# Early loads and early sums for the last product of a layer's last projection pair

## The chip, the cores and the metric

The kernel runs on one core of a Trainium2 chip. The metric is device time in microseconds (us) of one execution, shown as the median of several runs.

## The reference

Two layers of a streaming encoder on 512 tokens of width 2048, in float32:

```
def hybrid_layer(x, ...):
    h = rmsnorm(x, g_pre)
    z = h @ w_in                       # columns for a GLA group and an attention group
    o_gla = silu(gg) * rmsnorm(gla_chunk_causal(gq, gk, gv, log_a), g_gla)
    o_att = silu(ag) * rmsnorm(chunk_band_attention(aq, ak, av, rel_bias), g_att)
    y = concatenate([o_gla, o_att]) @ w_out
    return x + rmsnorm(y, g_post)
```

`reference` applies this twice. The change lies in `y = ... @ w_out` of the first layer, in its last two blocks of 512 columns, and so just ahead of the second layer's first projection.

## The kernel before

Weights come in blocks of 512 columns, each cut into eight chunks of 128 x 1024 float32 (512 KB). Every chunk is split into a rounded high half `wh` (cast on ScalarE, L200) and a low half `wl` (subtraction on VectorE, L209), so that three fast matmuls give nearly float32 accuracy.

Most blocks are multiplied in pairs by a Strassen-like scheme (`fast_gemm`): seven products P1 to P7 take the place of eight. Each product is a row of four jobs, one for each chunk index c from 0 to 3. A job is 12 matmuls of 128x512. The order in which the jobs run is written out by hand; for this pair it is `PROD_END`, where "20" is P2's job 0:

```
PROD_END = order("10 20 11 21 12 22 13 23 50 51 60 52 61 53 62 63 30 31 32 33 70 71 72 73 40 41 42 43")
```

A `Job` has three steps, each prepared some jobs ahead (`ahead`: up to five for loads, up to four for the others):

- `load` sends DMAs from SyncE's queue (SP). P1 loads into the ring `H` (4 buffers); P2, P5, P6 and, in this pair, P4 load into the ring `raw` (5 buffers). P5, P6, P3 and P7 also fetch an operand (a sum of activations, hi and lo half) into the ring `sa` (4 buffers), at L180. In the first layer's last pair (`mid`), P6 also loads the chunk that P7 will need into the slots `a110` to `a113`, under `p["t", c]`.
- `high` makes the weight combination on VectorE: `h = h + r` in place for P5, P6 and P4 (L194), `r = h - r` for P7 (L196). Then ScalarE casts the result to `wh`.
- `low` subtracts `wh` from it into `wl` (ring of 3 buffers).

`slot(tag, ...)` gives a named buffer that is held by one tile at a time; a new tile of the same tag waits for the last reader of the one before. P2's operands in this pair lie in the slots `a120`, `a121`, `g14` and `g15` (`OG` for p = 0): P2's jobs 0 to 3 read `g14`, `g15`, `a120`, `a121`.

The tile framework orders each engine's instructions ahead of time; `tc.issue_after(x)` puts an instruction behind x on its engine. Side work is written as generators that `pump` advances between jobs: in this stage `finish(0)` and `prep_half`. When P3 is complete, `finish_both` reduces the squares (L1372), takes the inverse root on GpSimd (L429), updates the residual rows on VectorE (L1383, four of them) and stores them to `x_mid`. `prep_half` then takes the squares (L442), reduces them (L443), scales the rows (L497, L499; its scaled rows lie in `g0`, `g14`, `g1`, `g15`), transposes them on TensorE (L513) and builds the second layer's operands. P4's last job is put behind the second group of transposes. The jobs behind P4 are the second layer's first block, of kind `std`; each loads one chunk into `raw`.

Of the kernel before, what the change touches and what calls it, by code (L numbers as in the profile page):

```python
# [11 lines left out]
ALU = mybir.AluOpType  # L12
# [11 lines left out]
NB_IN = 14  # L24
# [9 lines left out]
def hybrid_trunk(  # L34
# [13 lines left out]
    nc = tc.nc  # L48
# [16 lines left out]
    def nm(s):  # L65
        serial[0] += 1
        return f"{s}_{serial[0]}"

    def slot(tag, shape, dtype=F32):
        return slots.tile([P] + shape, dtype, tag=tag, name=nm(tag))  # L70

    def rtile(tag, shape=(2, W), dtype=F32, bufs=4):
        return ring.tile([P] + list(shape), dtype, tag=tag, name=nm(tag), bufs=bufs)
# [27 lines left out]
    def flat(t):  # L101
        return t.bitcast(F32).rearrange("p a b -> p (a b)")
# [30 lines left out]
    PROD_OUT = order("10 20 11 21 12 13 50 51 60 61 22 23 52 53 62 63 30 31 32 33 70 71 72 73 40 41 42 43")  # L133
    LEFT = {"P5": "S1", "P6": "S2", "P3": "S4", "P7": "S3", "P4": "A22"}
    SPARE = ("g12", "g13", "g16", "g17")
    lows, last_turn = [], [None]
    last_cast, last_low, last_mm, last_load, last_h = [None], [None], [None], [None], [None]

    class Job:
# [14 lines left out]
        def load(self):  # L154
            k, c, p, b0, b1 = self.kind, self.c, self.pair, self.b0, self.b1
            end = b0 >= NB_IN and k != "std"
            if end:
                c = OC[c]
            top, bottom = (c + 4, c) if end else (c, c + 4)
            mid = end and b0 == W23[0] and self.l < L - 1  # L160
            if k == "std":
                self.raw = self.fetch(rtile("raw", bufs=5), b0, c)
            elif k == "P1":
                p["H", self.c] = self.fetch(rtile("H"), b0, top)
                last_h[0] = last_load[0]
            elif k == "P5":
                p["r", self.c] = self.fetch(rtile("raw", bufs=5), b1, top)
            elif k == "P6":
                p["r", self.c] = self.fetch(rtile("raw", bufs=5), b1, bottom)
            elif k == "P7":  # L170
                p["r", self.c] = p.pop(("t", self.c), None) or self.fetch(rtile("raw", bufs=5), b0, top)
            elif k == "P2" or (k == "P4" and end):
                p["r", self.c] = self.fetch(rtile("raw", bufs=5), b0, bottom)
            sums = (so_d if end else sa_d)[self.l]
            src = sums.get((LEFT.get(k), c))
            if src is not None and b0 != NB_IN and not (k == "P5" and b0 == AV0):
                until(lambda: k == "P4" or (id(sums), LEFT[k], c) in written)
                self.a = rtile("sa", (2, 512), F32R)
                with tc.issue_after(last_h[0]) if mid else nullcontext():
                    last_load[0] = nc.sync.dma_start(flat(self.a), src).ins  # L180
            if b0 == W23[0] and k == ("P6" if mid else "P5"):
                with tc.issue_after(last_h[0]):
                    p["t", self.c] = self.fetch(slot(f"a11{self.c}" if mid else SPARE[self.c], [2, 512]), b0, c + 4)

        def high(self):
            k, c, p = self.kind, self.c, self.pair
            if k == "std":
                src = self.raw
            else:
                h, r = p["H", c], p.get(("r", c))  # L190
                src = h if k in ("P1", "P5", "P6", "P4") else r
                with tc.issue_after(lows[-2]) if self.b0 >= NB_IN else nullcontext():
                    if k in ("P5", "P6") or (k == "P4" and self.b0 >= NB_IN):
                        nc.vector.tensor_tensor(out=h, in0=h, in1=r, op=ALU.add)  # L194
                    elif k == "P7":
                        nc.vector.tensor_tensor(out=r, in0=h, in1=r, op=ALU.subtract)  # L196
            self.src = src
            self.wh = rtile("wh", dtype=F32R)
            for z in self.parts():
                last_cast[0] = nc.scalar.copy(self.wh[:, z, :], src[:, z, :]).ins  # L200
# [70 lines left out]
    def until(cond):  # L271
        while not cond():
            assert tasks or delayed
            pump(1)
# [1234 lines left out]
```

## Time and profile before

| | us |
|---|---|
| median of 3 runs | 1618.36 (1616.69 to 1619.23) |
| the profiled execution | 1617.52 |
| its span, first to last instruction | 1615.5 |

The page of the profile lists busy time by engine, a picture of the span in 40 slices, the chain of work that ended last and the costliest groups of instructions. A row of the timeline reads: start, duration, engine, line, operation, output<-input, form, count, and in brackets the idle time before it with what ended it. A row of stretches reads: stretch, its length, busy time (and instruction count) of PE (matmul), PEld (weight load), DVE (VectorE), ACT (ScalarE) and POOL (GpSimd), the granted TensorE clock, the DMA engines' busy share, and GB/s. A row of DMA issues gives the output and input, the queue, the count, the size of each and the median time from issue to landing. A row of waits gives total us, times, and the longest.

In this trace the first layer's last pair runs on PE from about 725 us (P1 and P2) over 747 (P5 and P6), 769 (P3), 780 (P7) and 791 (P4) to about 806 us.

### The profile page before, as it was taken

The numbers are of one execution on the slowest core, as the hardware profiler recorded it, in microseconds if no ns is written. First come the engines' busy times: TensorE is split into PE (matmuls) and PEld (weight loads), VectorE is DVE, ScalarE is ACT, GpSimd is POOL, SyncE is SP. The second block draws the span as 40 slices with busy tenths as digits, with TensorE's granted clock in tenths as the row PEclk, the third lists the DMA queues.
The fourth block names the chain that finished last, engine by engine and source line by source line (L and its number), as shares of the span: only waits on it lengthen the run. The fifth ranks groups of instructions, "written<-read, shape, count | busy, mean of one in ns | idle before, by whom it ended". The sixth has DMA issues, their size and how long they took to land.

```text
span 1615.5 us, 24476 instructions
## 1 busy us (share of the span) xinstructions
PE 1600.5 (99%) x8938; PEld 1372.8 (85%) x8938; DVE 1272.4 (79%) x1646; ACT 918.5 (57%) x1507; POOL 131.5 (8%) x192
## 2 busy tenths in 40 slices
PE   9999999999999999999999999999999999999997
PEld 7888999998888777888788889999988887788886
DVE  5977778678777878998988677786786878689887
ACT  7544445657455546665696444456675545566654
POOL 0120000010010010100122000000100100101001
PEclk9999999999999999999999999999999999999999
DMA  9797686685867768689779886867858687686986
GB/s 370 263 366 268 240 293 216 226 299 176 286 211 277 268 217 317 223 307 381 265 263 359 330 295 228 305 203 243 309 201 294 208 298 254 222 302 233 342 299 193
DMA packets 133928, 438.17 MB, mean 271 GB/s; under 512 B 14404, under 2 KB 27204, under 8 KB 133776
## 3 DMA queue, kind: packets, MB, share of 16 engines
q1 hardware_dynamic: 117072, 375.99, 66.9%
q0 software_dynamic: 16160, 59.53, 10.0%
q8 instruction: 71, 1.16, 0.3%
q10 hardware_dynamic: 576, 1.08, 0.2%
q14 instruction: 49, 0.40, 0.1%
HBM read 377.02 MB, written 61.62 MB: 272 GB/s over the span
## 4 chain that ended last, share of the span: by engine, by line
PE 94%; DVE 2%; DMA 1%; issue 1%; ACT 1%; POOL 0%; DVEq 0%; SPq 0%; ACTq 0%; POOLq 0%
PE mm L387 53%; PE mm L377 19%; PE mm L309 10%; PE ax L937 2%; PE ax L387 2%; PE ax L1123 1%; PE ax L920 1%; PE ax L744 1%; PE ax L1095 1%; DMA raw<-in_w_dram 1%; PE ax L900 1%; PE ax L899 1%; PE ax L898 1%; DVE wl L209 0%; DMA bias<-in_rel_dram 0%
## 5 line engine op out<-in xcount | busy, mean ns | idle before, releaser
L387 PE MATMUL mm<-wh,sa 128*128 128x512 f32 x1600 | 517.8, 394 | 0.8 <-ACT wh L200 0.5
L200 ACT CAST wh<-H 128x1024 fp32r<-128x1024 f32 x256 | 268.5, 1051 | 217.0 <-PE mm L387 91.6
L209 DVE TENSOR_TENSOR wl<-H,wh 128x1024 fp32r<-128x1024 f32 x256 | 312.3, 1221 | 94.6 <-PE mm L387 37.6
L387 PEld LDWEIGHTS mm<-wh,sa 128*128 128x128 f32 x1600 | 299.5, 188 | 73.0 <-issue 9.4
L200 ACT CAST wh<-raw 128x1024 fp32r<-128x1024 f32 (+1 forms) x233 | 244.1, 1052 | 197.0 <-PE mm L387 89.5
L209 DVE TENSOR_TENSOR wl<-raw,wh 128x1024 fp32r<-128x1024 f32 (+1 forms) x233 | 282.4, 1215 | 61.9 <-PE mm L387 24.5
L387 PE MATMUL mm<-wl,sa 128*128 128x512 f32 x800 | 312.6, 391 | 0.0
L377 PE MATMUL mm<-sa,wh 128*128 128x256 f32 x1280 | 237.4, 285 | 0.0
L387 PE MATMUL mm<-wh,a 128*128 128x512 f32 x640 | 211.5, 394 | 0.0
L377 PEld LDWEIGHTS mm<-sa,wh 128*128 128x128 f32 x1280 | 200.3, 191 | 0.3
L377 PE MATMUL mm<-sa,wl 128*128 128x256 f32 x640 | 180.9, 283 | 0.0
L387 PEld LDWEIGHTS mm<-wl,sa 128*128 128x128 f32 x800 | 150.3, 188 | 30.1 <-DVE wl L209 0.4
L194 DVE TENSOR_TENSOR H<-H,raw 128x1024 f32<-128x1024 f32 x144 | 174.9, 1219 | 1.0
L387 PEld LDWEIGHTS mm<-wh,a 128*128 128x128 f32 x640 | 119.5, 188 | 24.9
L387 PE MATMUL mm<-wl,a 128*128 128x512 f32 x320 | 125.6, 393 | 0.0
L377 PEld LDWEIGHTS mm<-sa,wl 128*128 128x128 f32 x640 | 122.5, 191 | 0.0
L429 POOL TENSOR_TENSOR sm<-sm,mhalf 128x2 f32<-128x2 f32 (+2 forms) x40 | 55.5, 1387 | 764.3 <-DVE sm L947 458.7
L196 DVE TENSOR_TENSOR raw<-H,raw 128x1024 f32<-128x1024 f32 x56 | 68.5, 1223 | 51.1 <-DMA raw<-in_w_dram 50.5
L387 PE MATMUL mm<-wh,g 128*128 128x512 f32 x320 | 101.6, 391 | 0.0
L377 PE MATMUL mm<-a,wh 128*128 128x256 f32 x512 | 95.4, 285 | 0.0
L339 ACT COPY ev<-mm 128x512 f32<-128x512 f32 x104 | 60.7, 584 | 60.2 <-PE mm L387 43.4
L215 DVE TENSOR_TENSOR H<-H,raw 128x1024 f32<-128x1024 f32 x48 | 58.7, 1223 | 35.7 <-DMA raw<-in_w_dram 35.4
(250 smaller groups left out, 2323.8 us busy)
## 6 DMA issues: line engine op xcount, KB each, us to landing
raw<-in_w_dram SPq DMA_DIRECT2D x311, 512.0 KB, 5.2
sa<-S SPq DMA_DIRECT2D x184, 512.0 KB, 4.5
H<-in_w_dram SPq DMA_DIRECT2D x64, 512.0 KB, 5.0
sa<-A SPq DMA_DIRECT2D x48, 512.0 KB, 5.8
S<-g POOLq DMA_DIRECT2D x32, 512.0 KB, 8.7
sa<-oS SPq DMA_DIRECT2D x32, 512.0 KB, 5.3
oS<-g POOLq DMA_DIRECT2D x16, 512.0 KB, 4.4
oS<-sa POOLq DMA_DIRECT2D x16, 512.0 KB, 5.6
```

The costliest lines, as they stand in the source:

```text
L194: nc.vector.tensor_tensor(out=h, in0=h, in1=r, op=ALU.add)
L196: nc.vector.tensor_tensor(out=r, in0=h, in1=r, op=ALU.subtract)
L200: last_cast[0] = nc.scalar.copy(self.wh[:, z, :], src[:, z, :]).ins
L209: last_low[0] = nc.vector.tensor_tensor(out=self.wl[:, z, :], in0=self.src[:, z, :], in1=self.wh[:, z, :].bitcast(F32), op=ALU.subtract).ins
L215: nc.vector.tensor_tensor(out=h, in0=h, in1=self.src, op=ALU.add)
L309: nc.tensor.matmul(pss[o], a(part, kk, o) if callable(a) else a[:, part, t], rhs[:, kk, :], start=(i == 0 and kk == 0 and m == 0), stop=(i ...
L339: nc.scalar.copy(e, src[t])
L377: nc.tensor.matmul(dst, lhs[:, kk, f], a[:, part, tok], start=(fresh and kk == 0 and m == 0 and ft % 2 == 0), stop=(c == 3 and kk == 1 and ...
L387: last_mm[0] = nc.tensor.matmul(out_ps[t], a[:, part, tok], rhs[:, kk, :], start=(fresh and kk == 0 and m == 0), stop=(c == 3 and kk == 1 ...
L429: nc.gpsimd.tensor_tensor(out=out_r, in0=v, in1=mhalf[:, : v.shape[-1]], op=ALU.pow)
L744: nc.tensor.matmul(ps[0:96, half * 256 : (half + 1) * 256], wga[kt // 10][:, kt % 10, :], op[:, i, (kt % 2) * 256 : (kt % 2 + 1) * 256], s ...
L937: nc.tensor.matmul(o, self.pt[i][:, j * P : (j + 1) * P], av[hd // 4, j // 2][:, j % 2, (hd % 4) * P : (hd % 4 + 1) * P], start=(j == 0), ...
```

## The change

P4's four chunk loads of the first layer's last pair no longer go to the ring `raw` with P4's jobs. They are issued with P3's jobs into the slots `a120`, `a121`, `g14` and `g15`, under `p["u", c]`. P4's sum `h + u` is issued right behind P7's difference in P7's `high`; P4's own `high` then only casts. The second layer's last pair and all other pairs stay as they were.

```
+    EARLY = ("a120", "a121", "g14", "g15")
...
-            elif k == "P2" or (k == "P4" and end):
+            elif k == "P2" or (k == "P4" and end and not mid):
                 p["r", self.c] = self.fetch(rtile("raw", bufs=5), b0, bottom)
+            if k == "P3" and mid:
+                p["u", self.c] = self.fetch(slot(EARLY[self.c], [2, 512]), b0, bottom)
...
-                    if k in ("P5", "P6") or (k == "P4" and self.b0 >= NB_IN):
+                    if k in ("P5", "P6") or (k == "P4" and self.b0 >= NB_IN and ("u", c) not in p):
                         nc.vector.tensor_tensor(out=h, in0=h, in1=r, op=ALU.add)
                     elif k == "P7":
                         nc.vector.tensor_tensor(out=r, in0=h, in1=r, op=ALU.subtract)
+                        if ("u", c) in p:
+                            nc.vector.tensor_tensor(out=h, in0=h, in1=p["u", c], op=ALU.add)
```

## The prediction

> **What bounds the kernel.** I read the page first: its busy shares and its chain.
>
> ```profile
> span 1615.5 us, 24476 instructions
> PE 1600.5 (99%) x8938; PEld 1372.8 (85%) x8938; DVE 1272.4 (79%) x1646; ACT 918.5 (57%) x1507; POOL 131.5 (8%) x192
> PE 94%; DVE 2%; DMA 1%; issue 1%; ACT 1%; POOL 0%; DVEq 0%; SPq 0%; ACTq 0%; POOLq 0%
> ```
>
> PE is busy for all but 15.0 us and carries 94% of the chain. A change that leaves the matmuls alone can win only idle PE time, and can lose by making PE wait. Next come the table of stretches around the last pair of the first layer, and the list of whom PE waited for in the whole run.
>
> ```profile
> 720.00:760.00 40.00, 40.00 (x177) 32.83 (x176) 32.30 (x34) 20.76 (x31) 0.00 (x0) 1.00 1.03 407
> 760.00:800.00 40.00, 38.81 (x171) 31.47 (x170) 34.83 (x37) 24.37 (x35) 6.77 (x10) 1.00 0.80 286
> 800.00:840.00 40.00, 39.46 (x199) 32.52 (x198) 36.05 (x54) 37.08 (x78) 8.65 (x15) 1.00 0.71 239
> ...
> PE mm L387 <- DVE wl L209: 1.2, 1, 1.2
> ...
> PE ax L513 <- ACT g L497: 0.4, 1, 0.4
> ```
>
> Two things matter. PE idles 1.19 + 0.54 = 1.73 us in the two later stretches, so the region offers less than 2 us and a little for pipeline restarts. And in the first stretch the DMA engines are full: share 1.03, 407 GB/s. The longest wait on a weight half (1.2 us) and the wait for L497 are the two that the change can touch. On PE they look like this:
>
> ```profile
> 793.93 0.62 PE L387 MATMUL mm<-wh,g 128*128 128x512 f32 x2
> 795.74 0.50 PE L387 MATMUL mm<-wl,g 128*128 128x512 f32 x1 [1.19 <-DVE wl L209]
> ...
> 800.63 0.39 PE L387 MATMUL mm<-wh,g 128*128 128x512 f32 x1
> 801.03 0.65 PE L513 MATMUL ax<-cst,g 128*128 128x128 f32 x4
> 802.07 1.53 PE L513 MATMUL ax<-cst,g 128*128 128x128 f32 x12 [0.38 <-ACT g L497]
> ```
>
> Back-to-back matmuls start 0.227 us apart (12 a job, so 2.72 us a job). Two from 793.93 would be followed at 794.38; the next starts at 795.74, so 1.36 us are lost in P4's second job. The transposes lose 0.17 us at 801.03 (after 800.63 + 0.23) and 0.6 us at 802.07 (four at 0.11 us end at 801.47). Together 2.1 us.
>
> **Part one: the sums move.** Four sums (L194) leave P4 and stand behind the four differences (L196).
>
> ```profile
> 769.19 1.22 DVE L209 TENSOR_TENSOR wl<-raw,wh 128x1024 fp32r<-128x1024 f32 x1 [1.48 <-PE mm L387]
> 770.33 1.22 DVE L196 TENSOR_TENSOR a<-H,a 128x1024 f32<-128x1024 f32 x1
> 771.91 1.23 DVE L209 TENSOR_TENSOR wl<-raw,wh 128x1024 fp32r<-128x1024 f32 x1 [0.36 <-issue]
> ...
> 786.65 0.15 DVE L1372 TENSOR_REDUCE sm<-ssy 128x1 f32<-128x5 f32 x1
> ...
> 789.67 1.28 DVE L1383 SCALAR_TENSOR_TENSOR g<-a,sm,g 128x1024 f32<-128x1024 f32 x1 [0.61 <-POOL sm L429]
> ...
> 794.46 1.22 DVE L209 TENSOR_TENSOR wl<-H,wh 128x1024 fp32r<-128x1024 f32 x1
> 795.60 1.22 DVE L194 TENSOR_TENSOR H<-H,raw 128x1024 f32<-128x1024 f32 x1
> 796.73 1.22 DVE L209 TENSOR_TENSOR wl<-H,wh 128x1024 fp32r<-128x1024 f32 x1
> 797.87 0.21 DVE L443 TENSOR_REDUCE sm<-sm 128x1 f32<-128x3 f32 x2
> ...
> 786.95 2.69 POOL L429 TENSOR_TENSOR sm<-sm,mhalf 128x2 f32<-128x2 f32 x1 [2.92 <-DVE sm L1372]
> 799.82 2.19 ACT L497 ACTIVATE g<-g,sm 128x1024 f32<-128x1024 f32 x2
> ```
>
> Each sum costs 1.14 us start to start. In the P3 jobs a low half and a difference take 2.28 of each 2.72 us, so a sum overfills a period by 0.70 us and DVE runs late by up to 4 x 0.70 = 2.8 us. That is covered: the low half at 771.91, done at 773.1, is for the job seven behind the one that starts at 758.28 (below), near 777.3, so 4.2 us ahead of use.
>
> What P4 wins is less than four sums. The late low half (794.46) stands behind four residual updates (L1383), which waited for POOL's 2.69 us; POOL had waited for the reduction at 786.65. Three of the four sums were ahead of the updates before; all four will be. In DVE's own time from 769.19 to 794.46 there is 3 x 0.36 + 0.61 = 1.7 us of idling, and one more sum (1.14) comes into it, so the low half could start at best 0.55 us earlier. That needs every gap filled. If the reduction stays near 786.65, POOL again releases the updates at 789.67 and nothing is won. I take 0, the nearer end: POOL's wait is the one that ended last. The other end is 0.55; all 1.36 would go only if DVE put the low half ahead of the updates.
>
> The sum at 795.60 does leave the way to the reduction at 797.87, which leads over POOL and L497 to the transposes. They can be 1.1 us earlier, more than the 0.77 lost there: gain 0.8 (0 if ACT is late instead). So P4 gives 0.8, bounds 0 and 2.1.
>
> **Part two: the loads move.** P4's four 512 KB loads no longer wait for raw buffers. They need P2's operand slots, and join the P3 jobs in program order. SP, however, sends a load when its buffer comes free, well ahead of program order:
>
> ```profile
> 755.74 1.22 DVE L194 TENSOR_TENSOR H<-H,raw 128x1024 f32<-128x1024 f32 x1
> ...
> 746.90 0.39 PE L387 MATMUL ax<-wh,a 128*128 128x512 f32 x1
> 747.12 0.62 PE L387 MATMUL mm<-wh,sa 128*128 128x512 f32 x2
> ...
> 758.05 0.62 PE L387 MATMUL mm<-wh,sa 128*128 128x512 f32 x2
> ...
> 747.06 0.33 SPq L457 DMA_DIRECT2D bias<-in_x_dram  x1
> 750.04 3.05 SPq L180 DMA_DIRECT2D sa<-oS  x2
> 753.43 0.33 SPq L151 DMA_DIRECT2D raw<-in_w_dram  x1
> 755.48 0.32 SPq L180 DMA_DIRECT2D sa<-oS  x1
> 756.99 0.33 SPq L151 DMA_DIRECT2D raw<-in_w_dram  x1
> ...
> 782.62 14.55 SPq L151 DMA_DIRECT2D raw<-in_w_dram  x4
> ```
>
> P4's first load went out at 756.99, 0.03 us after the sum that freed its buffer (755.74 + 1.22), though P4 ran on PE from about 791. P2's last matmul starts at 746.90, and its jobs alternate with P1's, so its slots come free near 730.8, 736.2, 741.7 and 747.1 (steps of two jobs). I expect all four loads on SP before 750.04, in the full stretch. Nothing leaves that stretch: the raw buffers which P4 gives up go to the next layer's first loads, at 756.99 and later (four of those leave 782.62). That is hidden, worth 0.
>
> What is queued behind them: the operand fetch (L180) at 750.04, for the fifth job of P5/P6, and the fetches and raw load behind it.
>
> ```profile
> sa<-oS SPq DMA_DIRECT2D x1, 512.0 KB, 7.3
> ...
> sa<-oS SPq DMA_DIRECT2D x1, 512.0 KB, 5.8
> ...
> 764.00:765.00 1.00, 1.00 (x6) 0.84 (x5) 1.00 (x1) 1.00 (x2) 0.00 (x0) 1.00 0.20 66
> ```
>
> The first row is the one DMA issued from 750 to 752: it lands at 757.3. PE needs it at 758.28 (second start of the row at 758.05). It has 0.9 us to spare. The engines are first free near 764. Four loads are 2.10 MB, at 407 GB/s 5.15 us, so the fetch lands 5.15 us later and PE waits 4.2 us, with 0.1 us of restart 4.3. The next fetch, the second row, goes out near 752.8 and lands at 758.6 for a job at 761.0: 2.4 to spare, plus the 4.3 that PE has then lost, against 5.15. So it is paid once. Bounds: 0 (the loads sent behind these fetches) and 5.2 (no slack left). I take 4.3, as the SP rows show eager sending.
>
> The Trainium skill (DMA: Bandwidth & Descriptors, Specifications) gives 358 GB/s as a core's HBM limit; the row's 407 exceeds it and decides. At 358 the four loads would take an estimated 5.9 us and PE would wait about 5.
>
> **Sum.** The profiled execution took 1617.52 us, 2.0 around its span; the median of the runs is 1618.36, 0.84 above. 4.3 - 0.8 = +3.5 us: 1621.0 in that execution's terms, 1621.9 as a median.
>
> **Rivals.**
> - *The clock drops.* A PE pause of four microseconds may cost more than itself.
>
> ```profile
> 1.18 4.23 PE L674 MATMUL ax<-t 128*128 128x512 bf16 x10 [1.18 <-DVE t L671]
> 6.41 1.19 PE L309 MATMUL mm<-wh,sa 128*128 128x512 f32 x4 [1.00 <-ACT wh L200]
> ```
>
> The first ten matmuls after the start run 0.42 us apart, against 0.227 later; after a pause of 1.0 us they are fast. If the new pause brings the slow state back for ten matmuls, it adds 10 x 0.19 = 2.0 us: 1623.9. Against: no pause in this trace is that long, and the granted clock reads 1.00 throughout. The Trainium skill (TensorE: Matmul & The Clock Gate, Why this matters for your kernels) warns of matmul gaps above about 3 us; by that rule this rival would hold, and no row here tests it.
> - *The loads are hidden: not slower.* If SP sends them behind the four fetches that end at 758.47 in the trace, into the free time from 764, PE waits for none of them. Deciding point: 0.9 us of slack is less than one load (1.29 us), so none may go ahead of the fetch at 750.04. Then only P4's gain is left, 0.8, up to 2.1 with the low half moved ahead: 1617.6 to 1616.3. For it: the loads are written into P3's jobs. Against: 756.99.
> - *The rest is reordered.* Orders are made for the whole program, so new free times may shift instructions in the second layer. Faster by over 3.2 us needs this, as the region holds 2.1; the whole run has 15.0 us of idle PE. Say 4 us either way: 1614.4 or 1625.9, the latter with the forecast's loss.
>
> **Chances.** 0.2% is 3.2 us, about what a measurement of this kernel can tell from no change: 1615.1 to 1621.6. Forecast 0.45 (1620.3 to 1623.5, of which 0.31 above 1621.6); clock 0.13; hidden 0.21; reordered faster 0.13, slower 0.08. Slower 0.31 + 0.13 + 0.08 = 0.52; same 0.14 + 0.21 = 0.35; faster 0.13. The range leaves out most of the reordered cases: 1615.9 to 1625.8. Its lower end is the hidden case with all 2.1 and 0.4 of run spread, its upper one 5.2 of waiting, 2.0 of clock and 0.2 of spread.
>
> **What would show it.** Right: four loads from the weights into a and g slots before the fetch near 750; that fetch landing past 760; a new PE wait of about 4 us on DMA sa near 758; sums between the differences; the updates still ahead of P4's second low half; no wait at the transposes. Wrong: no PE wait near 758, DMA landings unchanged, or PE idling elsewhere.

## The result and the profile after

| | median, us | runs | ratio to before, 95% interval |
|---|---|---|---|
| before | 1618.12 (1616.69 to 1619.23) | 6 | |
| the change | 1625.75 (1624.45 to 1627.39) | 6 | 1.0049 [1.0036, 1.0062] |

The change is slower by 7.6 us, between 5.8 and 10.0 by the interval. The prediction was +3.5: the sign is right, but the forecast is less than half of what was measured. The profiled execution of the change took 1627.39 us, the slowest of its six, so between the two traces lie 9.9 us, not 7.6. The account below is of these 9.9.

The page and the list of waits of the changed kernel, then the table of stretches (columns as before: PE, PEld, DVE, ACT, POOL, granted clock, DMA share, GB/s). Each kernel has its own line numbers: the matmuls L387 are L392 in the change, the weight half L209 is L214, the transposes L513 are L518.

```profile
span 1625.4 us, 24478 instructions
PE 1606.2 (99%) x8938; PEld 1376.1 (85%) x8938; DVE 1271.7 (78%) x1646; ACT 919.8 (57%) x1507; POOL 128.3 (8%) x192
...
PE mm L392 <- DMA sa<-oS: 4.5, 1, 4.5
PE ax L518 <- ACT g L502: 2.8, 1, 2.8
...
760.00:770.00 10.00, 7.64 (x27) 6.17 (x28) 5.18 (x5) 3.89 (x5) 0.00 (x0) 0.83 0.86 330
800.00:810.00 10.00, 7.25 (x33) 5.72 (x32) 8.23 (x11) 9.85 (x17) 3.38 (x7) 0.86 0.60 231
810.00:820.00 10.00, 10.00 (x49) 8.49 (x48) 7.88 (x15) 10.00 (x26) 0.87 (x4) 0.80 0.48 159
764.00:765.00 1.00, 1.00 (x3) 0.75 (x3) 0.20 (x1) 0.00 (x0) 0.00 (x0) 0.50 1.03 410
```

Three things are read from this. The matmuls are the same in number (8938), yet PE was busy 5.7 us longer and the span grew by 9.9: some of the loss is pause, some is matmuls that ran slowly. The 1.2 us wait on a weight half is gone from the list of waits; a wait for the operand fetch (DMA sa) is new, and the wait for L502 (before: L497) grew from 0.4 to 2.8 us. And the granted clock, 1.00 in all three stretches before, is below 0.9 behind each of the two pauses; in the single microsecond from 764 it is 0.50.

PE's timeline at the two places:

```profile
757.46 0.40 PE L392 MATMUL mm<-wh,sa 128*128 128x512 f32 x1
762.36 0.47 PE L392 MATMUL mm<-wh,sa 128*128 128x512 f32 x1 [4.50 <-DMA sa<-oS]
...
766.30 0.40 PE L392 MATMUL mm<-wl,sa 128*128 128x512 f32 x1
...
796.69 0.39 PE L392 MATMUL mm<-wh,g 128*128 128x512 f32 x1
...
804.63 0.39 PE L392 MATMUL mm<-wh,g 128*128 128x512 f32 x1
807.77 3.86 PE L518 MATMUL ax<-cst,g 128*128 128x128 f32 x16 [2.75 <-ACT g L502]
811.28 0.77 PE L392 MATMUL mm<-wh,g 128*128 128x512 f32 x1
...
814.25 0.39 PE L392 MATMUL mm<-wl,g 128*128 128x512 f32 x1
```

The row at 796.69 is P4's first matmul. In the kernel before it was this one:

```profile
790.92 0.40 PE L387 MATMUL mm<-wh,g 128*128 128x512 f32 x1
```

The account of the 9.9 us, against back-to-back starts (0.227 us a matmul, 0.11 a transpose):

| place | lost before | lost after | difference |
|---|---|---|---|
| pause at P6's second job (757.69 to 762.36) | 0 | 4.67 | +4.7 |
| ten intervals behind it, 762.36 to 766.30 = 3.94, at full speed 2.27 | 0 | 1.67 | +1.7 |
| P4's first three jobs, 36 matmuls, at full speed 8.17: 790.92 to 800.86 before, 796.69 to 804.86 after | 1.77 | 0 | -1.8 |
| pause at the transposes (804.86 to 807.77) | 0.77 | 2.91 | +2.1 |
| 16 transposes, 807.77 to 811.28 = 3.51, at full speed 1.75; seven intervals to 814.25 = 2.97, at full speed 1.59 | 0 | 3.14 | +3.1 |
| sum | 2.5 | 12.4 | +9.8 |

That is within 0.1 us of the 9.9. Of P4's 1.77 us, 1.36 were the stall at the second low half. So 5.0 us come at the operand fetch and the transposes as pure waiting after P4's gain is taken off, and 4.8 us as slow clock behind them.

**The operand fetch.** SP's queue and the landing of the fetch, from the timeline and the DMA issues of 753 to 754 us:

```profile
739.04 0.33 SPq L152 DMA_DIRECT2D g<-in_w_dram  x1
741.67 0.33 SPq L152 DMA_DIRECT2D g<-in_w_dram  x1
746.85 0.33 SPq L152 DMA_DIRECT2D a<-in_w_dram  x1
751.98 0.33 SPq L152 DMA_DIRECT2D a<-in_w_dram  x1
753.27 1.61 SPq L183 DMA_DIRECT2D sa<-oS  x2
...
sa<-oS SPq DMA_DIRECT2D x1, 512.0 KB, 9.0
```

All four early loads stand ahead of the fetch, which leaves at 753.27 in place of 750.04 and takes 9.0 us in place of 7.3: it lands at 762.3, and PE starts at 762.36.

**The transposes.** VectorE, GpSimd and ScalarE on the way to them:

```profile
777.36 1.23 DVE L201 TENSOR_TENSOR H<-H,a 128x1024 f32<-128x1024 f32 x1
...
787.59 0.69 DVE L349 TENSOR_TENSOR t<-mm,ev 128x512 f32<-128x512 f32 x1
789.32 1.22 DVE L201 TENSOR_TENSOR H<-H,g 128x1024 f32<-128x1024 f32 x1
792.19 0.69 DVE L349 TENSOR_TENSOR t<-mm,ev 128x512 f32<-128x512 f32 x1
795.73 0.15 DVE L1377 TENSOR_REDUCE sm<-ssy 128x1 f32<-128x5 f32 x1
796.74 1.22 DVE L214 TENSOR_TENSOR wl<-H,wh 128x1024 fp32r<-128x1024 f32 x1 [0.85 <-PE mm L392]
797.88 1.28 DVE L1388 SCALAR_TENSOR_TENSOR g<-a,sm,g 128x1024 f32<-128x1024 f32 x1
...
796.03 0.71 POOL L434 TENSOR_TENSOR sm<-sm,mhalf 128x2 f32<-128x2 f32 x1 [2.93 <-DVE sm L1377]
...
804.88 0.15 DVE L448 TENSOR_REDUCE sm<-sm 128x1 f32<-128x3 f32 x1 [0.94 <-ACT t L447]
...
806.57 2.19 ACT L502 ACTIVATE g<-g,sm 128x1024 f32<-128x1024 f32 x2
```

Three of the four sums (L201, the first and the last of the four shown) stand ahead of both of P3's last results (L349), and the fourth ahead of the second. The reduction of P3's squares (L1377) therefore comes at 795.73, 1.0 us ahead of P4's first matmul (796.69); before, at 786.65, it was 4.3 us ahead of it (790.92). VectorE then takes P4's third low half (796.74, which waits for a `wl` buffer to be read) ahead of the first residual update (797.88): 1.2 us behind P4's start, against 1.25 us ahead of it before. So, counted from P4's start, the updates come 2.4 us later. The rest of the chain is shorter than before: from the end of the last update to the second reduction it is 2.1 us (802.74 to 804.88) against 3.3 (794.55 to 797.87). The scaling therefore starts 9.9 us behind P4's first matmul (806.57) against 8.9 before (799.82), only 1.0 us later.

PE, on its side, reaches the transposes 8.17 us behind P4's first matmul against 9.94 before, because P4's stalls are gone. That adds up to the longer pause: 1.8 us are P4's old stalls, now waited out at the transposes, 1.0 us is the lateness of the chain, and 0.6 us that PE lost between the transposes before (ahead of 802.07) comes off. One order of VectorE makes both: P4's low halves are early because they went ahead of the updates. What P4 won at its low half was not kept, and the slow clock came on top.

### The profile page after: what moved, and what is told of

It is laid out like the page before. It is cut to its first block, busy times and chain, and to the rows that moved or that the text cites. A ratio compares the mean times of both kernels' runs of the same rounds, so it can differ in the third digit from the quotient of the medians.

```text
span 1625.4 us, 24478 instructions
## 1 busy us (share of the span) xinstructions
PE 1606.2 (99%) x8938; PEld 1376.1 (85%) x8938; DVE 1271.7 (78%) x1646; ACT 919.8 (57%) x1507; POOL 128.3 (8%) x192
## 4 chain that ended last, share of the span: by engine, by line
PE 94%; DMA 2%; DVE 2%; issue 1%; ACT 0%; DVEq 0%; SPq 0%; ACTq 0%
PE mm L392 52%; PE mm L382 20%; PE mm L314 10%; PE ax L942 2%; PE ax L392 2%; DMA raw<-in_w_dram 1%; PE ax L1128 1%; PE ax L925 1%; PE ax L749 1%; PE ax L1100 1%; DVE wl L214 1%; PE ax L905 1%; PE ax L904 1%; PE ax L903 1%; PE ax L518 1%
## 5 line engine op out<-in xcount | busy, mean ns | idle before, releaser
L392 PE MATMUL mm<-wh,sa 128*128 128x512 f32 x1600 | 519.3, 395 | 5.0 <-DMA sa<-oS 4.5
L214 DVE TENSOR_TENSOR wl<-H,wh 128x1024 fp32r<-128x1024 f32 x256 | 312.1, 1221 | 94.5 <-PE mm L392 34.4
L392 PEld LDWEIGHTS mm<-wh,sa 128*128 128x128 f32 x1600 | 300.2, 188 | 77.8 <-issue 8.3
L214 DVE TENSOR_TENSOR wl<-raw,wh 128x1024 fp32r<-128x1024 f32 (+1 forms) x233 | 282.4, 1215 | 65.7 <-PE mm L392 30.3
L392 PE MATMUL mm<-wl,sa 128*128 128x512 f32 x800 | 313.3, 392 | 0.1
L392 PE MATMUL mm<-wh,a 128*128 128x512 f32 x640 | 211.5, 394 | 0.0
L392 PEld LDWEIGHTS mm<-wl,sa 128*128 128x128 f32 x800 | 150.8, 188 | 30.8 <-DVE wl L214 1.1
L197 DVE TENSOR_TENSOR H<-H,raw 128x1024 f32<-128x1024 f32 x140 | 170.0, 1219 | 2.3 <-DMA raw<-in_w_dram 1.4
L392 PEld LDWEIGHTS mm<-wh,a 128*128 128x128 f32 x640 | 119.5, 188 | 24.9
L392 PE MATMUL mm<-wl,a 128*128 128x512 f32 x320 | 125.8, 393 | 0.0
L434 POOL TENSOR_TENSOR sm<-sm,mhalf 128x2 f32<-128x2 f32 (+2 forms) x40 | 52.5, 1314 | 759.0 <-DVE sm L952 457.7
L392 PE MATMUL mm<-wh,g 128*128 128x512 f32 x320 | 102.3, 393 | 0.0
L220 DVE TENSOR_TENSOR H<-H,raw 128x1024 f32<-128x1024 f32 x48 | 58.7, 1223 | 38.7 <-DMA raw<-in_w_dram 38.5
```

What stands on the lines that cost most here:

```text
L214: last_low[0] = nc.vector.tensor_tensor(out=self.wl[:, z, :], in0=self.src[:, z, :], in1=self.wh[:, z, :].bitcast(F32), op=ALU.subtract).ins
L220: nc.vector.tensor_tensor(out=h, in0=h, in1=self.src, op=ALU.add)
L392: last_mm[0] = nc.tensor.matmul(out_ps[t], a[:, part, tok], rhs[:, kk, :], start=(fresh and kk == 0 and m == 0), stop=(c == 3 and kk == 1 ...
L434: nc.gpsimd.tensor_tensor(out=out_r, in0=v, in1=mhalf[:, : v.shape[-1]], op=ALU.pow)
```

## The experiments

Theory A, put up after the result: two separate causes add up. The four loads delay the fetch by the time of their bytes (about 4.5 us and a clock drop behind it), and the four sums delay P3's results and with them the transposes. Its rivals: one cause behind both (all of it the loads, with the sums at nothing or a gain), and loads that cost little if they leave later. The texts below were written before each run. Each comparison is with runs of the kernel before beside it, with medians of 1618.12 us beside the change, 1617.82 beside the next four kernels and 1618.01 beside the last three.

| run | median, us | ratio to before, 95% interval | over before, us | PE idle in 700 to 900, us | granted clock of the run |
|---|---|---|---|---|---|
| before | 1617.82 to 1618.12 | | | 1.7 | 0.998 |
| the change | 1625.75 | 1.0049 [1.0036, 1.0062] | +7.6 | 7.3 | 0.995 |
| loads_only | 1623.34 | 1.0035 [1.0022, 1.0047] | +5.5 | 6.2 | 0.997 |
| sums_only | 1619.20 | 1.0007 [0.9998, 1.0016] | +1.4 | 3.0 | 0.997 |
| two_early | 1622.06 | 1.0025 [1.0016, 1.0035] | +4.2 | 5.2 | 0.997 |
| late_loads | 1620.76 | 1.0016 [1.0007, 1.0025] | +2.9 | 3.6 | 0.997 |
| one_sum | 1615.45 | 0.9986 [0.9977, 0.9995] | -2.6 | 0.7 | 0.998 |
| two_sums | 1615.39 | 0.9983 [0.9975, 0.9992] | -2.6 | 0.5 | 0.998 |
| free_last | 1619.17 | 1.0002 [0.9993, 1.0011] | +1.2 | 1.9 | 0.998 |

The idle column is 200 us less PE's busy time in the profiled execution (before 198.27); the last column is the median over all runs of a kernel.

**loads_only: the loads early, the sums where they were.**

```
-                        if ("u", c) in p:
-                            nc.vector.tensor_tensor(out=h, in0=h, in1=p["u", c], op=ALU.add)
...
-                    if k in ("P5", "P6") or (k == "P4" and self.b0 >= NB_IN and ("u", c) not in p):
-                        nc.vector.tensor_tensor(out=h, in0=h, in1=r, op=ALU.add)
+                    if k in ("P5", "P6") or (k == "P4" and self.b0 >= NB_IN):
+                        nc.vector.tensor_tensor(out=h, in0=h, in1=p.get(("u", c), r) if k == "P4" else r, op=ALU.add)
```

> P4's four chunks load early into P2's operand slots as in the change, but the sums stay in P4's own high step. Theory A (two separate losses: the loads take about 5 us of full DMA ahead of an operand fetch, and the moved sums push the residual chain back): the PE wait near 757 on the operand fetch stays at 4.5 us, with about 1.7 us of half clock behind it, and P4 looks as it did before the change (1.2 us wait on the low half, under 1 us at the transposes): 5.5 to 6.5 us above the kernel before. Theory B (one loss, the late fetch; the transposes wait only because that pause shifted everything behind it): the same first wait and also the 2.8 us wait at the transposes, 7 to 8 us above. Theory C (the sums alone lose, the loads are covered): within 1 us of the kernel before.

Measured +5.5 us. Its waits, and the stretch behind the first:

```profile
PE mm L390 <- DMA sa<-oS: 4.5, 1, 4.5
PE mm L390 <- DVE wl L212: 1.2, 1, 1.2
PE ax L516 <- ACT g L500: 0.4, 1, 0.4
...
760.00:770.00 10.00, 8.36 (x30) 6.83 (x31) 5.13 (x5) 4.61 (x6) 0.00 (x0) 0.83 0.78 296
```

The fetch costs the same 4.5 us as in the change, the two waits of the kernel before are back at their old size, and the clock drops behind the 4.5 us pause again. So the first cause needs no moved sum, and the longer wait at the transposes does.

**sums_only: the sums early, the loads through `raw` again.** SP then sends the loads when raw buffers come free, as before.

```
-                p["u", self.c] = self.fetch(slot(EARLY[self.c], [2, 512]), b0, bottom)
+                p["u", self.c] = self.fetch(rtile("raw", bufs=5), b0, bottom)
```

> The sums stand behind P7's differences as in the change, but P4's chunks load into the ring raw, as they did before. Theory A: no PE wait near 757, P4's 1.2 us wait on the low half gone, and a wait of 2 to 3 us at the transposes, with or without a drop of the clock: 0.5 to 4 us above the kernel before. Theory B: no wait at the transposes, 1 to 2 us below the kernel before. Theory C: about 7.5 us above.

Measured +1.4 us, with an interval that takes in zero.

```profile
PE ax L518 <- ACT g L502: 3.0, 2, 2.8
...
788.90 0.15 DVE L1377 TENSOR_REDUCE sm<-ssy 128x1 f32<-128x5 f32 x1
...
789.87 0.39 PE L392 MATMUL mm<-wh,g 128*128 128x512 f32 x1
...
800.00:810.00 10.00, 8.81 (x48) 7.69 (x49) 8.84 (x12) 10.00 (x22) 0.93 (x1) 0.83 0.40 126
```

There is no wait for the fetch and none above 0.3 us for a low half, and the wait at the transposes has grown as in the change, with a lower clock behind it. The reduction (788.90) is again 1.0 us ahead of P4's first matmul (789.87). The forecast had a gain of 0.8 here. Loads alone and sums alone add to 6.9 of the change's 7.6, which fits two causes that hardly touch each other; the intervals (2 us either way for the loads, 1.5 for the sums) could not show a small overlap.

**two_early: two loads ahead of the fetch in place of four.** All else as in the change.

```
-            if k == "P3" and mid:
+            if k == "P3" and mid and self.c >= 2:
                 p["u", self.c] = self.fetch(slot(EARLY[self.c], [2, 512]), b0, bottom)
...     (behind the operand fetch of P3's own load)
+            if k == "P3" and mid and self.c < 2:
+                with tc.issue_after(last_load[0]):
+                    p["u", self.c] = self.fetch(slot(EARLY[self.c], [2, 512]), b0, bottom)
```

> Two of the four chunks (P4's jobs 2 and 3) load early as in the change, the other two behind P3's operand fetches; the sums as in the change. By the arithmetic of the full DMA (1.29 us a load, 0.9 us of slack) the operand fetch lands 2.6 us later and PE waits 1.6 to 2.0 us near 757 in place of 4.5. If a pause under about 3 us keeps the granted clock at 1.00, no matmul behind it runs at half rate, and the time falls by more than the wait does: against the changed kernel 4 to 5 us faster. If the pause does not follow the number of loads, the late fetch has another cause.

Measured 3.7 us below the change (3.4 if each is set against its own runs of the kernel before), a little less than expected; the wait of 2.1 us is a little more.

```profile
PE ax L521 <- ACT g L505: 3.1, 2, 2.8
PE mm L395 <- DMA sa<-oS: 2.1, 1, 2.1
...
760.00:770.00 10.00, 10.00 (x46) 8.24 (x45) 6.73 (x6) 5.70 (x7) 0.00 (x0) 1.00 0.98 363
800.00:810.00 10.00, 6.86 (x42) 5.51 (x42) 8.24 (x13) 10.00 (x22) 1.64 (x2) 1.00 0.55 196
```

This is the dose: 0 (sums_only), 2 and 4 loads ahead of the fetch make PE wait 0, 2.1 and 4.5 us. By the prediction's sum (2 x 1.29 less 0.9 of slack) it is 1.7, and 4.2 for four. After a pause of 2.1 us the clock stays at 1.00, so this half also takes away the 1.7 us of slow matmuls. The profiled execution (1620.10 us) is the fastest of nine and the only one with a mean clock of 0.998; the other eight have 0.996 or 0.997. In those the clock most likely drops somewhere, as it does in sums_only; where, no trace of them shows.

**late_loads: all four loads behind P3's operand fetches.** The same edit as in two_early, for all four (`k == "P3" and mid`).

> The change, with each early load held on SP behind the operand fetch of the same P3 job, so that none stands ahead of P5's and P6's fetches. Theory A: no PE wait near 757; VectorE's order comes out a little different from the changed kernel's (P3's results and the residual updates stand further ahead), so the transposes wait less than 2.8 us: 2 us below to 2 us above the kernel before. Theory B: 1 to 2 us below the kernel before. If the loads are then late for the sums, VectorE waits on DMA near 771 to 780, and PE for a low half.

Measured +2.9 us: neither the old waits nor no change.

```profile
781.61 0.47 PE L393 MATMUL mm<-wh,sa 128*128 128x512 f32 x1 [0.68 <-DMA sa<-oS]
...
795.69 0.50 PE L393 MATMUL mm<-wh,g 128*128 128x512 f32 x1 [2.92 <-ACT ev L345]
...
794.03 1.05 ACT L448 ACTIVATE t<-g 128x1024 bf16<-128x1024 f32 x1
795.08 0.56 ACT L345 COPY ev<-mm 128x512 f32<-128x512 f32 x1
...
790.00:800.00 10.00, 7.08 (x26) 5.38 (x25) 9.17 (x11) 8.47 (x14) 3.28 (x7) 0.85 0.54 211
```

Here VectorE's order puts the residual updates ahead of P4's low halves, and in ScalarE's order the squares (L448), which need the updated rows, stand ahead of the copy (L345) of P7's last result. P4's first job needs the PSUM buffer which that copy empties, so PE waits 2.9 us at P4's start and the clock drops (0.85). There is no wait near 758 and none for L503 at the transposes, as expected. The 0.7 us at 781.61 are another fetch, for P7's first job: the loads now leave between 762 and 771 us, the DMA share of 766 to 770 us rises from 0.79 to 1.00, and the fetch sent at 772.80 takes 8.7 us, where the one sent at 772.07 before took 5.4. The time lies above the expected 2 us all the same, because the text allowed for a new order on VectorE but not on ScalarE; a load's new place shifts both.

**one_sum and two_sums: only the first, or the first two, of the four sums early; loads through `raw`.** sums_only with this, and the same with `self.c < 2`:

```
-            elif k == "P2" or (k == "P4" and end and not mid):
+            elif k == "P2" or (k == "P4" and end and not (mid and self.c < 1)):
...
-            if k == "P3" and mid:
+            if k == "P3" and mid and self.c < 1:
```

> The kernel before, with only the sum of P4's job 0 moved behind P7's first difference; loads stay in the ring raw. Theory (the loss of the moved sums is their place ahead of P3's results; one sum fits the gaps that VectorE had there): the second reduction of P3's results, the four residual updates, P4's second low half and the transposes all come about 1 us earlier against P4 than before, so the 1.2 us wait on the low half falls under 0.5 us and the transposes wait less than 0.3 us: 1 to 2 us below the kernel before. Rival (any sum moved ahead of P3's results delays the chain): reductions later by about 1 us, transposes wait 1 to 2 us, 0 to 2 us above the kernel before.

> As one_sum, with the sums of P4's jobs 0 and 1 moved. Theory: the second sum no longer fits a gap, it delays P3's results by about 1 us and spares the same later: like one_sum within 1 us. Rival: 1 us more loss than one_sum.

Measured -2.6 us for both; both are faster than the kernel before by intervals that leave out 1, and faster than the change by 10 us. VectorE and PE in one_sum:

```profile
785.10 0.15 DVE L1377 TENSOR_REDUCE sm<-ssy 128x1 f32<-128x5 f32 x1
...
792.42 1.22 DVE L214 TENSOR_TENSOR wl<-H,wh 128x1024 fp32r<-128x1024 f32 x1
...
790.83 0.39 PE L392 MATMUL mm<-wh,g 128*128 128x512 f32 x1
793.54 0.62 PE L392 MATMUL mm<-wh,g 128*128 128x512 f32 x2
794.00 0.39 PE L392 MATMUL mm<-wl,g 128*128 128x512 f32 x1
...
800.03 1.53 PE L518 MATMUL ax<-cst,g 128*128 128x128 f32 x12 [0.38 <-ACT g L502]
```

The reduction is 5.7 us ahead of P4's start (785.10, 790.83), against 4.3 before, and the second low half (792.42) is done 0.35 us ahead of its use (794.00): the 1.36 us are gone. The 0.38 us wait at the transposes stayed, which the expectation had put under 0.3. In two_sums the reduction is 5.5 us ahead (786.74, 792.25), in sums_only 1.0: the third and fourth sum are what pushes P3's results back. From P4's first matmul to the second layer's first, PE took 15.00 us in one_sum (790.83 to 805.83) and 15.02 in two_sums, against 16.95 before (790.92 to 807.87). So 1.95 of the 2.6 us are shown here, 1.36 at the low half and the rest in smaller gaps of P4's jobs and ahead of the transposes. The interval (0.8 to 3.7 us for one_sum) holds 1.95, and where the rest lies, if it is real, stays open.

**free_last: sums_only without the rule that P4's last job goes behind the second group of transposes.**

```
-            with tc.issue_after(half_turns[1]) if (k, c) == ("P4", 3) and half_turns else nullcontext():
+            with nullcontext():
```

> sums_only (all four sums moved, loads in the ring raw) without the rule that puts P4's last job behind the second layer's second group of transposes. Theory (the wait of 2.8 us comes from that rule together with the later residual chain): PE runs P4's last job in that time, the wait and the half clock behind it go, but the first block of the second layer waits for its operands, which are made no earlier: 0.5 to 2 us of new wait before the first L314 matmuls; together 0 to 2 us below sums_only. Rival: the whole wait of 2.8 us only moves to the first L314 matmuls, time as sums_only within 0.5 us.

Measured +1.2 us, with an interval that takes in zero: the time of sums_only within 0.5 us, as the rival had it, though its whole wait did not move to the L314 matmuls.

```profile
PE ax L518 <- ACT H L529: 1.3, 1, 1.3
PE ax L518 <- ACT g L502: 0.4, 1, 0.4
...
800.00:810.00 10.00, 8.09 (x47) 5.92 (x46) 9.05 (x12) 10.00 (x22) 0.93 (x1) 1.00 0.53 185
```

With a job to run in between, the one wait of 2.8 us becomes two of 0.4 and 1.3 at the two groups. The clock stays up (0.998 in all eleven runs), and still the time is not better. ScalarE is busy for the whole ten microseconds here, as it was before, and both waits are for it. So it looks as if ScalarE set the pace here, whatever PE does in between; no run lightens ScalarE, so this is not shown.

## Why the prediction was right and wrong

Step by step, as the prediction has them:

- *SP sends the four loads ahead of the fetch.* Right, in order and in consequence. Only the time was later: the last left at 751.98, not before 750.04, since every load sent also delays the next: from 746.85 to 753.27 the sends of the change follow each other 1.28 us apart.
- *"PE waits 4.2 us, with 0.1 us of restart 4.3."* Right: 4.5 us of wait, 4.67 from start to start. The slack of 0.9 us and 1.29 us a load gave the dose of two_early too (1.7, measured 2.1). The wait was paid once, as forecast. The Trainium skill (DMA: Bandwidth & Descriptors, Specifications) would have made it an estimated 5 us by its 358 GB/s; the stretch at 764 moved 410 GB/s, and the measured wait lies between the two sums.
- *"Nothing is won" at P4's low half.* Wrong: all 1.36 us went. The text named the condition, VectorE putting the low half ahead of the updates, and left it out of the sum; this is what happened.
- *"They can be 1.1 us earlier ... gain 0.8"* at the transposes. **This is the step that failed.** It followed the one sum that left the end of the chain (795.60) and not the four that were put at its head. The 1.1 us were there: last update to second reduction fell from 3.3 to 2.1 us. But the prediction held the reduction "near 786.65". The four sums, 0.70 us over each period, made VectorE late by 2.8 us, which the text had worked out itself, but it set this only against the next low half and not against P3's results queued behind on the same engine. In the run the reduction moved from 4.3 us ahead of P4 to 1.0 us ahead, and the scaling came 1.0 us later, not 1.1 earlier, while PE arrived 1.8 us sooner. In place of -0.8 stand +2.1 us of pause and P4's -1.8, together about +0.4, and 3.1 us of slow clock. The sums alone cost 1.4 us in the median (sums_only, an interval that takes in zero) where -0.8 was forecast.
- *The clock drops* was a rival at 0.13 with 2.0 us, and stood at nothing in the sum. **This is the term that was most wrong:** it held twice, 1.7 us behind the fetch, close to the price, and 3.1 us behind the transposes, where no pause was expected, 4.8 of the 6.4 us that lie between the forecast and the trace. That no pause in the trace before was as long stood as a reason against it; it only meant that this trace could not tell. All six runs of the change have a mean clock of 0.994 to 0.996, against 0.998 or 0.999 in all 25 runs of the kernel before that stood beside loads_only; 0.003 of 1620 us is 4.9 us, the 4.8 of the account. The rule that the prediction cited (the Trainium skill, TensorE: Matmul & The Clock Gate, Why this matters for your kernels) warns of gaps above about 3 us. The 4.5 us pauses agree with it; drops also followed pauses of 2.75 to 2.92 us, though not each of them.
- *The loads are hidden* was priced at no wait for SP sending them behind the fetches. late_loads made that order: the wait near 758 was gone, but 0.7 us at a later fetch and 2.9 us at P4's start came with it. The deciding point was right, the price was not.

The total: +3.5 = 4.3 - 0.8 became, in the profiled execution, 4.7 + 1.7 for the loads and 2.1 + 3.1 - 1.8 for the sums. The term for the loads' wait was sized well; the sign of the sums' term and the clock were not.

## What to carry to other kernels

When work is put earlier on an in-order engine, follow what stands behind it on that engine to its last consumer, not only the work that it left; here 2.8 us of VectorE's lateness, which its next consumer could bear, fell on a reduction several steps ahead of the transposes. A stall that goes is a gain only if PE does not meet the same chain again a little later. A load sent early on a full queue delays the fetch behind it by about its bytes over the rate, so count the slack of the next fetch in loads (here 0.9 us, less than one). Where a move helps in part, try a smaller dose: one sum of four gave the gain of the move (1.95 us from P4 on) without its cost.

## What the runs showed of the hardware beyond that

- **Pauses and the clock.** In the stretch that the change touches, the nine traces hold five drops of the granted clock to 0.50, read here in steps of 0.1 us. Four of them last 3.4 us (behind the 4.5 us pauses of the change and loads_only, the 2.77 us of sums_only and the 2.92 us of late_loads) and cost up to 1.7 us; the fifth, behind the 2.75 us pause of the change, lasts 6.8 us, twice as long (807.2 to 814.1). The drop need not begin at the pause: in late_loads it begins 1.3 us after PE's restart (796.9 against 795.69). Between 2.75 and 2.92 us it went either way, with none behind the 2.76 us of two_early; of the eleven runs of sums_only, two keep the mean clock of 0.998 and nine do not. None followed pauses of 1.2 (loads_only), 1.3 (free_last) or 2.1 us. What decides whether it comes, and its length, was not tried.
- **GpSimd.** The inverse root (L434) took 0.71 us in the change and 2.69 before, for the same 128x2 input. It was on the way to the updates in both, and made up 2.0 of the 3.3 us by which the change's reduction was later against P4. What makes the difference stays open.
